# Which slot of the big pool a new tile takes: the order of the program against the times of the plan

## The chip, the cores and the metric

The kernel runs on one core of one Trainium2 chip. A core has a matrix engine (TensorE, PE in the profile, with its weight loads as PEld), three engines for elementwise work (VectorE or DVE, ScalarE or ACT, GpSimd or POOL), and SyncE (SP), which here only issues DMAs. Each engine works through its own list of instructions in the order in which they were written, and they wait for each other by semaphores. Times are microseconds (us) of the device for one execution; the figure that counts is the median over several executions. For the kernel before it is 727.84 us, from three runs between 727.78 and 729.07 us.

## The reference

One layer of a hybrid decoder on 1024 tokens of width 1024, all in float32:

```
h  = rmsnorm(x) * (1 + scale(c)) + shift(c)
cv, cg, cs, lx, ls = split(h @ w_in)                 # five blocks of 1024
v  = causal_depthwise_conv(cv * sigmoid(cg), 31 taps)
y_conv = (silu(layernorm(v)) @ pw2_w + pw2_b) * silu(cs)
xs = causal_depthwise_conv(lx, 4 taps)
r, i = sigmoid(xs @ wr + br), sigmoid(xs @ wi + bi)  # block-diagonal, 8 heads
a  = exp(-8 * r * softplus(-lam))
hs = scan: h_t = a_t h_{t-1} + sqrt(1 - a_t^2) (i_t xs_t)
y_lru = hs * silu(ls)
x  = x + (1 + gate(c)) * (concat(y_conv, y_lru) @ w_out)
out = rmsnorm(x)
```

The change leaves all of this as it is.

## The kernel before

The activations lie transposed in the on-chip memory, 128 channels by 1024 tokens to a tile of 512 KB, so each of x, v, the conv results and so on is eight tiles. A float32 product is made of three matmuls: both operands are split into a rounded part and a remainder (names with `hi` or `h`, and `lo` or `l`), and high*high, high*low and low*high are added up.

The stages follow each other in PE's list: the first four column blocks of `h @ w_in` while the inputs still arrive (`first`), the other 36 blocks with the block-diagonal gates among them (`ps`, `gate`), the lru half of `w_out` (`lp`, `lx`, `ly`), the layer norm over the convolution, the products with `pw2` (`xpw`, `zpw`, `ypw`) and with the conv half of `w_out` (`xout`, `zout`, `yout`, `y`), the last two in a scheme with seven products instead of eight. Beside this run the convolutions: five of the eight channel tiles are accumulated by DVE (`cacc`, `caccs`), three are made of products by ACT (`cq`, `co`) which GpSimd adds into `es` and `oo` with accumulating DMAs. Such DMAs also make remainders of weights and add the lru half of the output to a copy of x in HBM (`accd<-acc`).

**The plan.** Nothing is issued while the kernel text runs through these stages. Each operation is first noted in a list (class `Plan`, `op`, line 190), with its engine, an estimated cost, a priority and the buffers that it reads and writes. `Plan.order` (line 219) then plays the list through: at each planned time an engine that is free takes the ready operation of the smallest priority number, on condition that the pools have room for the buffers that it uses for the first time. A pool counts its free places in `free`. A place is taken when an operation that first uses a buffer is taken, and comes back at the planned end of the buffer's last operation (`releases`, line 255). For a DMA that end is the planned landing. `order` returns pairs of planned start and operation, sorted by planned start.

**The slots.** `Plan.run` (line 332) goes through that order. At the first use of a buffer it asks the pool of the framework for a tile, then it issues the operation. The big pool (line 351) has 47 slots of 128x1024 float32 under one tag, and the framework hands out the slot that has been unused longest in program order. 485 buffers go through these 47 slots. The plan counts how many slots are free at a planned time; which one a buffer gets is the framework's choice. The first instruction that writes a tile waits, by a semaphore, for the instructions and DMAs that last used the tile that lay in the slot before. Waits of this kind are the only thing that the choice of a slot decides.

What goes through the big pool: x, its scaled halves `uh` and `ul`, the modulation weights `modw`, all tiles of the conv and lru paths, the products `cq` and `co`, the split operands (`vha`, `vla`, `yha` and so on), the weights of the lru stage (`whi`, `wlo` from `w_out`), the combined weights of the last stages (`h34pw`, `l34pw`, ...), the running sums `acc` and `fin` and the outputs `o`. The weights of the 36 column blocks have pools of their own with two slots a name (`raw`, `whi`, `wlo`), and so have the small tiles and the accumulators of PE.

Lines that the profile names: 541 and 717 issue the matmuls of the products, 1400 those of the lru quarters, 386 and 394 the instructions of ACT, 405, 413 and 427 those of DVE, 418 GpSimd's accumulating DMAs, 432 the loads and stores of SP, 437 the stores of the output.

Of the kernel before, what the change touches and what calls it, by code (L numbers as in the profile page):

```python
# [38 lines left out]
NBIG = 47  # L39
# [60 lines left out]
FINP = -0.5  # L100
BCLATE = False
BEHIND = 0
TERMS = {**{("pw2_0", c): ("HW", "X") for c in "1z"}, **{(f"out_{p}", "1"): ("HX", "W") for p in (0, 1, 2, 3)}, **{(f"pw2_{p}", "1"): ("HX", "W") for p in (1, 2, 3)}}
LTERMS = {}
LLATE = 45
# [51 lines left out]
class Plan:  # L157
# [172 lines left out]
        return out  # L330

    def run(self):
        for _, o in self.order():
            for b in o.bufs:
                if b.tile is None:
                    pool, tag, shape, _ = self.pools[b.pool]
                    b.tile = pool.tile(shape, b.dtype, tag=tag, name=b.name)
            o.emit()

# [2 lines left out]
def hymba_layer(ctx: ExitStack, tc: tile.TileContext, xT, vecs, mod_w, w_first, w_in,  # L342
# [3 lines left out]
    act, dve, pool, pe, sp = nc.scalar, nc.vector, nc.gpsimd, nc.tensor, nc.sync  # L346
# [1 line left out]
    const = ctx.enter_context(tc.tile_pool(name="const", bufs=1))  # L348
    wpool = ctx.enter_context(tc.tile_pool(name="wpool", bufs=2))
    gwp = ctx.enter_context(tc.tile_pool(name="gwp", bufs=2))  # L350
    big = ctx.enter_context(tc.tile_pool(name="big", bufs=NBIG))
    small = ctx.enter_context(tc.tile_pool(name="small", bufs=2))
    psum = ctx.enter_context(tc.tile_pool(name="psum", bufs=3, space=bass.MemoryType.PSUM))
    psacc = ctx.enter_context(tc.tile_pool(name="psacc", bufs=2, space=bass.MemoryType.PSUM))
# [25 lines left out]
    def ACT(prio, out, in_, func, n=T, bias=None, scale=None, accum=None, r=(), w=(),  # L380
            reserve=0, after=()):
        kw = {}

        def emit():
            if func == "copy":
                act.copy(out(), in_())  # L386
                return
            if bias is not None:
                kw["bias"] = bias
            if scale is not None:  # L390
                kw["scale"] = scale
            if accum is not None:
                kw["accum_out"] = accum
            act.activation(out=out(), in_=in_(), func=func, **kw)  # L394
        ptr = sum(x is not None and not isinstance(x, float) for x in (bias, scale))
        return S.op("ACT", a_cost(n, ptr) + (0.1 if accum is not None else 0), emit, prio, r, w,
                    table=SETS.get(func), reserve=reserve, after=after)
# [26 lines left out]
    def TS(prio, out, a, s1, s2, op0, op1=None, r=(), w=(), n=0, after=()):  # L424
        kw = {} if op1 is None else {"op1": op1}
        return S.op("DVE", d_cost(n) if n else 0.2,
                    lambda: dve.tensor_scalar(out=out(), in0=a(), scalar1=s1, scalar2=s2, op0=op0,
                                              **kw), prio, r, w, after=after)
# [11 lines left out]
    def big_buf(name, dt=F32, parts=1):  # L440
        return S.buf("big", name, dt, parts)

    def part(b, a, e):
        return lambda: b()[:, a:e]

    def halves(b, a, e):
        return [(b, i) for i in range(b.parts) if i * (T // b.parts) < e
                and a < (i + 1) * (T // b.parts)]
# [7 lines left out]
    def vec(name, t):  # L456
        o = OFF[name] + t
        return V[:, o:o + 1]
# [21 lines left out]
    slots = list(FIRST + NEXT)  # L480
# [52 lines left out]
    def mm_k(prio, ps, s, xh, xl, k, cols, off=0, first=0, final=KT - 1, after=(), group="HXW", end=True):  # L533
        wh, wl = whi[s], wlo[s]
        at = LK.index(k) if s[0] == "lru" else k
        terms = [{"H": (wh, xh), "X": (wh, xl), "W": (wl, xh)}[t] for t in group]

        def emit():
            for i, (lhs, rhs) in enumerate(terms):
                for a, b in cols:  # L540
                    pe.matmul(ps()[:, a - off:b - off], k3(lhs)()[:, at, :], rhs[k]()[:, a:b],  # L541
                              start=(k == first and lhs is wh and rhs is xh
                                     and (a - off) % H == 0),
                              stop=(k == final and end and i == len(terms) - 1), skip_group_check=True)
        n = sum(b - a for a, b in cols)
        rd = [(wh, at)] * ("H" in group or "X" in group) + [(wl, at)] * ("W" in group)
        wr = []
        for a, b in cols:
            for x, ts in ((xh, "HW"), (xl, "X")):
                if any(t in group for t in ts):  # L550
                    rd += halves(x[k], a, b)
            wr += halves(ps, a - off, b - off)
        return S.op("PE", len(terms) * sum((b - a + 32) / 2400 for a, b in cols), emit, prio, rd, wr, after=after, columns=len(terms) * n)
# [6 lines left out]
    def acc_tile(name):  # L560
        return S.buf("acc", name, F32)
# [137 lines left out]
    def pair_products(name, n, w, sets, use, orders=(ORDER7,), apart=0):  # L699
# [7 lines left out]
        def product(a, b, ps, start):  # L707
            (wh, wl), xs, made = w[a], sets[b], products[name, c]
            groups = TERMS.get((name, c), ("HXW",))
            order = [(g, j) for g in groups for j in range(len(xs))]  # L710
# [128 lines left out]
    def fw_mm(prio, ps, i, xh, xl, k, cols, after=(), off=0, z=None):  # L839
        _, wh, wl = fw[k - k % 2]  # L840
        terms = ((wh, xh, 0), (wl, xh, 0), (wh, xl, 1))
        if z is not None:
            terms = terms[z:z + 1]

        def emit():
            for lhs, rhs, last in terms:
                for a, b in cols:
                    pe.matmul(ps()[:, a - off:b - off], fw_part(lhs, k, i * P, i * P + P)(),  # L848
                              rhs()[:, a:b], start=k == 0 and lhs is wh and rhs is xh,
                              stop=k == KT - 1 and bool(last), skip_group_check=True)  # L850
        n = sum(b - a for a, b in cols)
        rd, wr = [], []
        for lhs, rhs, _ in terms:
            rd.append((lhs, k % 2))
            for a, b in cols:
                rd += halves(rhs, a, b)
        for a, b in cols:
            wr += halves(ps, a, b)
        return S.op("PE", len(terms) * sum((b - a + 32) / 2400 for a, b in cols), emit, prio, rd, wr, after=after, columns=len(terms) * n)

    low = {}
    for i, ld in enumerate(LOADS):
        p = due[ld] = i - 100.0
# [5 lines left out]
        elif ld[0] in "wW":  # L869
            nk = 1 + (ld[0] == "W")  # L870
            rw, hi, lo = fw[k - k % 2]
            n, o, js = nk * FW, (k % 2) * FW, range(k % 2, k % 2 + nk)
# [17 lines left out]
    def col(t, j):  # L890
        return t[:, j:j + 1]
# [26 lines left out]
    for k in range(KT):  # L918
        p = due[f"s{k}"]
# [3 lines left out]
        else:  # L923
            dot(SCALE[k], p, KT + k, [gs_op])
        gs_op = S.op("DVE", 0.2, lambda k=k, a_=a_: dve.scalar_tensor_tensor(
            out=col(gs, k), in0=a_, scalar=col(b1, k), in1=vec("norm_g", k), op0=ALU.add,
            op1=ALU.mult), p, [("macc", KT + k), ("b1", 0)], [("gs", k)], lock=True)
        p = max(p, due[f"x{k}"], due[f"w{k}"])
# [4 lines left out]
        for a, e in START if k < UK else ((0, T),):  # L933
            n = e - a
            hk = halves(x_, a, e)
            if k == 0 == a:
                o = first_u = TS(p, part(uh, a, e), part(x_, a, e), g, None, ALU.mult, n=n,
                       r=hk + [("gs", k)], w=halves(uh, a, e))
            else:
                o = ACT(p, part(uh, a, e), part(x_, a, e), AF.Copy, n, scale=g,  # L940
                        r=hk + [("gs", k)], w=halves(uh, a, e))
# [7 lines left out]
        for ch, z in ((ch, z) for ch in (0, 1) for z in range(3 if k < ZK else 0)):  # L949
            for i, ps in enumerate(psf):  # L950
                if START[ch] in cuts[i]:
                    o = fw_mm(p + 0.1 * ch, ps, i, uh, ul, k, START[ch:ch + 1], z=z)
                    last_u[k, i, ch] = o
        for ch, (a, e) in enumerate(START):
            for i, ps in enumerate(psf):
# [3 lines left out]
                o = fw_mm(q, ps, i, uh, ul, k, ((a, e),))  # L959
# [3 lines left out]
    for k in range(KT):  # L963
        p = SQP + k
# [3 lines left out]
        for i, j in SQPAIR.get(k, ()):  # L968
            a, b = sqs[i], sqs[j]
# [33 lines left out]
    for k in range(KT):  # L1003
        p = due[f"h{k}"]
# [3 lines left out]
            out=col(shift, k), in0=a_, in1=vec("mod_shift_b", k), op=ALU.add), p,  # L1008
# [29 lines left out]
    for ch, (a, e) in enumerate(START):  # L1038
        for k in range(KT):
            p, n = TP + k + HCH * ch, e - a  # L1040
# [59 lines left out]
    held = []  # L1100
# [371 lines left out]
    for i, (s, ps) in enumerate(zip(FIRST, psf)):  # L1472
        j, p, bi = s[1] % KT, EVP + i, bias[:, i:i + 1]
        t = big_buf(f"first_u{i}", parts=4)
        for a, e in START:
            tk, pk, n = halves(t, a, e), halves(ps, a, e), e - a
# [3 lines left out]
            else:  # L1480
                late = acc_tile("late")
# [18 lines left out]
    n, started, pending_evac = 3, {}, {}  # L1500
    for s in slots[4:]:
# [41 lines left out]
        for gr, k in [(gr, k) for gr in groups for k in range(KT)]:  # L1543
            o = mm_k(n, ps, s, xh, xl, k, FULL, group=gr, end=gr == groups[-1])
# [11 lines left out]
        if s[0] == "in":  # L1556
            if s in NEXT:
                t, i = big_buf(f"next{n}", parts=2), len(FIRST) + NEXT.index(s)
# [4 lines left out]
            else:  # L1563
                o = evac_in(m, ps, n)
# [4 lines left out]
        else:  # L1569
            t = big_buf(f"acc{m}")  # L1570
# [10 lines left out]
    begun_pw2, last = [], [started[n - 1], started[n]]  # L1581
    for p in range(KT // 2):
        n = C0 + 2 * p
# [26 lines left out]
        last = [ops[0], ops[3]]  # L1610
# [5 lines left out]
    acc, n = {}, D0  # L1616
# [67 lines left out]
    for p, wout, apart in zip(OUT_P, WOUT, APART):  # L1684
        end = p == OUT_P[-1]
        n = D0 + 2 * p
        pw[p] = w = pair_weights("out", p, n, last[:1], last[1:], wout)
        n = D0 + NOUT[p]
# [17 lines left out]
        last = [ops[LASTS[p][0]], ops[LASTS[p][1]]]  # L1706
# [6 lines left out]
    n = D0 + 6  # L1713
    for prios, z, (a, e) in zip(ENDP, NPE, END[1:]):
        last_block(prios, a, e)
        norm(z, a, e)
    for o in scalings[END[1][0]][len(scalings[END[1][0]]) - BEHIND:]:
        S.hold(o, inverse[END[2][0]])
# [57 lines left out]
```

## Time and profile before

| | |
|---|---|
| runs, median | 727.84 us (727.78, 727.84, 729.07) |
| the profiled execution, its own time | 728.6 us |
| its span, first to last instruction | 726.8 us |
| granted clock of TensorE, mean | 0.996 |
| PE busy | 717.4 us (99%) |
| DVE busy | 616.5 us (85%) |
| ACT busy | 481.0 us (66%) |
| POOL busy | 170.9 us (24%) |
| DMA | 137.80 MB, mean 190 GB/s |

The profiled execution is 0.8 us longer than the median of the runs, and 1.8 us of its time lie outside of its span. A line of the waits names the engine and tile that waited, behind the arrow what ended the wait, then the total in us, the number of waits and the longest. A line of the timeline has the start, the duration, the engine, the source line, the operation with output and inputs, and in brackets the idle time of the engine before it with what ended it. Names have their buffer numbers left out, so `vla` stands for vla0 to vla3.

### The profile page before, as it was taken

To read this page: it belongs to the slowest core of one execution; us is meant where nothing else is said; L and a number is where in the kernel's file an instruction comes from. 1 tells how busy PE (TensorE), PEld (TensorE's weight loads), DVE (VectorE), ACT (ScalarE), POOL (GpSimd) and SP (SyncE) were. 2 spreads that over 40 slices of the span, in tenths; PEclk is the share of its full clock that TensorE was granted. 3 is DMA by queue.
4 is the path that set the end of the run, shared out by engine and by line. 5 is a ranking of instruction groups with operands and counts; after the bars stand their busy time and mean duration, and the time that the engine had idled before them with its cause. 6 is when DMAs were issued, how large, how long until landed. Compare 5 with 4: busy or idle time off the path is not lost.

```text
span 726.8 us, 9080 instructions
## 1 busy us (share of the span) xinstructions
PE 717.4 (99%) x3274; PEld 596.6 (82%) x3274; DVE 616.5 (85%) x848; ACT 481.0 (66%) x615; POOL 170.9 (24%) x172
## 2 busy tenths in 40 slices
PE   8999999999999999999999999999999999999996
PEld 7888888888888888888888888878888888888885
DVE  6999999889779999689499985999779766999646
ACT  7650679654779767966949779868785345745322
POOL 0035223343534230232220220111120101100003
PEclk9999999999999999999999999999999999999998
DMA  9946338758798998799999587998856946774006
GB/s 337 407 150 181 51 95 231 209 118 199 168 222 196 272 227 215 178 221 216 192 203 319 106 174 168 260 234 245 195 94 109 287 112 137 235 187 178 25 15 216
DMA packets 46059, 137.80 MB, mean 190 GB/s; under 512 B 5200, under 2 KB 15824, under 8 KB 45904
## 3 DMA queue, kind: packets, MB, share of 16 engines
q0 software_dynamic: 20016, 54.84, 42.0%
q1 hardware_dynamic: 24992, 81.48, 32.1%
q10 hardware_dynamic: 1008, 0.92, 0.4%
q8 instruction: 25, 0.41, 0.2%
q14 instruction: 18, 0.15, 0.1%
HBM read 79.37 MB, written 21.50 MB: 139 GB/s over the span
## 4 chain that ended last, share of the span: by engine, by line
PE 88%; ACT 4%; DVE 3%; issue 2%; DMA 1%; SPq 0%; DVEq 0%; ACTq 0%
PE ps L541 50%; PE xout L717 6%; PE xpw L717 6%; PE first L848 5%; PE ypw L717 3%; PE gate L1268 2%; PE lp L541 2%; PE lx L1400 2%; PE y L687 2%; PE zout L717 1%; PE zpw L717 1%; PE ly L541 1%; PE lx L541 1%; PE yout L717 1%; PE lp L1400 1%
## 5 line engine op out<-in xcount | busy, mean ns | idle before, releaser
L541 PE MATMUL ps<-uh,whi 128*128 128x512 f32 x576 | 177.4, 389 | 0.0
L541 PE MATMUL ps<-ul,whi 128*128 128x512 f32 x576 | 177.3, 389 | 0.0
L541 PE MATMUL ps<-uh,wlo 128*128 128x512 f32 x576 | 177.3, 389 | 0.0
L541 PEld LDWEIGHTS ps<-ul,whi 128*128 128x128 f32 x576 | 108.1, 188 | 22.5
L541 PEld LDWEIGHTS ps<-uh,wlo 128*128 128x128 f32 x576 | 108.1, 188 | 22.4
L541 PEld LDWEIGHTS ps<-uh,whi 128*128 128x128 f32 x576 | 108.0, 188 | 22.4
L386 ACT CAST whi<-raw 128x1024 fp32r<-128x1024 f32 (+1 forms) x44 | 45.1, 1031 | 44.1 <-PE ps L541 27.7
L418 POOL DMA_DIRECT2D es<-cq x45 | 41.0, 911 | 128.3 <-ACT cq L394 81.9
L413 POOL TENSOR_TENSOR wlo<-raw,whi 128x1024 fp32r<-128x1024 f32 x16 | 41.6, 2606 | 89.8 <-ACT whi L386 89.6
L394 ACT ACT_TABLE_LOAD x45 | 57.7, 1283 | 6.2 <-issue 2.5
L405 DVE SCALAR_TENSOR_TENSOR cacc<-v,V,cacc 128x511 f32<-128x511 f32 (+14 forms) x75 | 55.6, 741 | 0.5
L405 DVE SCALAR_TENSOR_TENSOR caccs<-v,V,caccs 128x511 f32<-128x511 f32 (+6 forms) x70 | 52.0, 743 | 2.2 <-ACT caccs L394 1.1
L405 DVE SCALAR_TENSOR_TENSOR caccs<-c,wsum,caccs 128x511 f32<-128x511 f32 (+6 forms) x70 | 52.0, 742 | 0.8
L418 POOL DMA_DIRECT2D oo<-co x39 | 37.0, 980 | 45.3 <-issue 11.9
L394 ACT ACTIVATE cq<-v,V 128x511 f32<-128x511 f32 (+14 forms) x45 | 31.7, 707 | 0.0
L405 DVE SCALAR_TENSOR_TENSOR modw<-modw,sc 128x1024 f32<-128x1024 f32 x23 | 29.5, 1286 | 2.1 <-DMA modw<-in_mod_w_dram 2.1
L405 DVE SCALAR_TENSOR_TENSOR xs<-ps,V,xs 128x1023 f32<-128x1023 f32 (+2 forms) x24 | 30.6, 1275 | 0.0
L413 DVE TENSOR_TENSOR wlo<-raw,whi 128x1024 fp32r<-128x1024 f32 x20 | 24.4, 1219 | 6.5 <-ACT whi L386 6.3
L394 ACT ACTIVATE cq<-c,wsum 128x512 f32<-128x512 f32 x42 | 29.6, 712 | 0.0
L394 ACT ACTIVATE co<-v,V 128x510 f32<-128x510 f32 (+12 forms) x39 | 26.9, 706 | 0.0
L394 ACT ACTIVATE finsq<-fin 128x512 f32<-128x512 f32 (+2 forms) x14 | 7.9, 570 | 27.6 <-DVE fin L405 14.4
L413 POOL TENSOR_TENSOR o<-fin,bc 128x256 f32<-128x256 f32 (+1 forms) x8 | 7.8, 996 | 68.1 <-ACT bc L386 68.1
(413 smaller groups left out, 1582.2 us busy)
## 6 DMA issues: line engine op xcount, KB each, us to landing
raw<-in_w_in_dram SPq DMA_DIRECT2D x36, 512.0 KB, 5.8
modw<-in_mod_w_dram SPq DMA_DIRECT2D x24, 512.0 KB, 9.2
scsd<-scs SPq DMA_DIRECT2D x8, 512.0 KB, 4.5
raw<-in_w_out_dram SPq DMA_DIRECT2D x8, 512.0 KB, 7.7
accd<-acc POOLq DMA_DIRECT2D x8, 512.0 KB, 7.3
rawpw<-in_pw_dram SPq DMA_DIRECT2D x8, 512.0 KB, 4.6
scsr<-scsd SPq DMA_DIRECT2D x8, 512.0 KB, 4.5
rawout<-in_w_out_dram SPq DMA_DIRECT2D x8, 512.0 KB, 3.5
```

The lines of the kernel that those rows point to most:

```text
L386: act.copy(out(), in_())
L394: act.activation(out=out(), in_=in_(), func=func, **kw)
L405: dve.scalar_tensor_tensor(out=out(), in0=in0(), scalar=scalar, in1=in1(), op0=op0, op1=op1, accum_out=accum)
L413: lambda: e.tensor_tensor(out=out(), in0=a(), in1=b(), op=op), prio, r, w,
L418: return S.op("POOL", ISSUE, lambda: pool.dma_start(out(), a(), accum_op=ALU.add), prio, r, w, lag=RATE * n / T, after=after, flight=flight)
L541: pe.matmul(ps()[:, a - off:b - off], k3(lhs)()[:, at, :], rhs[k]()[:, a:b], start=(k == first and lhs is wh and rhs is xh and (a - off) % ...
L687: pe.matmul(to(), half(*lhs)()[:, j * P:j * P + P], half(*rhs)()[:, c0:c1], start=a == "S1" and j == 0 and t == 0, stop=j == KT // 2 - 1 a ...
L717: pe.matmul(half(ps, 0)(), half(*lhs)()[:, j * P:j * P + P], half(*rhs)(), start=start and at == 0 and i == 0, stop=at == len(order) - 1 a ...
L848: pe.matmul(ps()[:, a - off:b - off], fw_part(lhs, k, i * P, i * P + P)(), rhs()[:, a:b], start=k == 0 and lhs is wh and rhs is xh, stop=k ...
L1268: pe.matmul(ps()[:, c0:c1], lhs()[:, j, :], rhs()[:, c0:c1], start=st == 0, stop=st == 2)
L1400: pe.matmul(half(ps, h)(), lhs()[:, o:o + P], half(*rhs)(), start=begin and j == 0 and t == 0, stop=j == NJ - 1 and t == 2, skip_group_che ...
```

## The change

The order of the operations stays as the plan makes it. `Plan.run` now picks the slot itself for the pools named in `PLACED`, which is the big pool alone. The pool is opened with one slot a tag, and 47 tags (`big0` to `big46`) take the place of 47 slots under one tag.

A first pass over the order notes for each buffer the place of its last operation in program order, the latest planned end of its operations, and that same end with `MARGINS` = 2.0 us added for DMAs (operations of SP, and GpSimd's accumulating DMAs, which have a `lag`). In the second pass the first 47 buffers take the tags in turn. Each later one looks at the slots whose holder has its last operation earlier in program order. Among these, slots whose holder has ended by the planned start of the operation go first, and among equals the one with the earliest noted end.

```
+PLACED = ("big",)
+MARGINS = 2.0
...
     def run(self):
-        for _, o in self.order():
+        out = self.order()
+        last, slots = {}, {p: [] for p in PLACED}
+        for i, (_, o) in enumerate(out):
+            for b in o.bufs:
+                late = MARGINS if o.lag or o.eng == "SP" else 0.0
+                _, end, far = last.get(b, (0, 0.0, 0.0))
+                last[b] = (i, max(o.end, end), max(o.end + late, far))
+        for i, (t, o) in enumerate(out):
             for b in o.bufs:
                 if b.tile is None:
-                    pool, tag, shape, _ = self.pools[b.pool]
+                    pool, tag, shape, cap = self.pools[b.pool]
+                    if b.pool in PLACED:
+                        held = slots[b.pool]
+                        if len(held) < cap:
+                            held.append(b)
+                            n = len(held) - 1
+                        else:
+                            n = min((z for z in range(cap) if last[held[z]][0] < i),
+                                    key=lambda z: (last[held[z]][1] > t, last[held[z]][2]))
+                            held[n] = b
+                        tag = f"{tag}{n}"
                     b.tile = pool.tile(shape, b.dtype, tag=tag, name=b.name)
             o.emit()
...
-    big = ctx.enter_context(tc.tile_pool(name="big", bufs=NBIG))
+    big = ctx.enter_context(tc.tile_pool(name="big", bufs=1))
```

## The prediction

> **What bounds the kernel now.** I read the page's totals first, then the busy time by stage, then PE's waits, and only then the waits of the other engines. The page:
>
> ```profile
> span 726.8 us, 9080 instructions
> PE 717.4 (99%) x3274; PEld 596.6 (82%) x3274; DVE 616.5 (85%) x848; ACT 481.0 (66%) x615; POOL 170.9 (24%) x172
> PE 88%; ACT 4%; DVE 3%; issue 2%; DMA 1%; SPq 0%; DVEq 0%; ACTq 0%
> ```
>
> PE holds 88% of the chain that ended last. A busy share of 99% alone doesn't say that PE runs at its pace, so the chain in order of time and the busy time by stage come next (columns there: length, then busy time and count of PE, PEld, DVE, ACT, POOL, the granted clock, the DMA share and rate):
>
> ```profile
> 120.58 81.60 PE ps L541 x360
> ...
> 0.00:12.70 12.70, 10.85 (x58) 9.41 (x58) 6.22 (x18) 8.34 (x13) 0.70 (x6) 1.00 0.86 304
> 12.70:60.00 47.30, 47.28 (x223) 39.31 (x224) 46.67 (x78) 27.43 (x40) 11.60 (x5) 1.00 0.78 294
> 60.00:414.00 354.00, 354.00 (x1571) 293.36 (x1570) 315.56 (x426) 253.28 (x318) 112.89 (x111) 1.00 0.81 190
> 414.00:475.00 61.00, 61.00 (x271) 50.40 (x269) 49.72 (x54) 53.55 (x57) 13.42 (x16) 1.00 0.86 198
> 475.00:520.00 45.00, 44.61 (x212) 36.86 (x211) 39.70 (x43) 30.82 (x38) 6.14 (x7) 1.00 0.90 239
> 520.00:717.20 197.20, 197.17 (x930) 165.25 (x929) 154.10 (x222) 106.19 (x148) 22.62 (x24) 1.00 0.55 141
> 717.20:726.80 9.60, 2.50 (x18) 2.04 (x17) 4.56 (x12) 1.39 (x5) 3.51 (x5) 0.72 0.65 219
> ```
>
> 360 matmuls in 81.60 us are 226.7 ns each, without a gap over seven column blocks. From 12.70 to 717.20 us PE's idle time is 0.02 + 0 + 0 + 0.39 + 0.03 = 0.44 us, at a granted clock of 1.00. So in 704.5 us of the span a change of waits can win 0.44 us. PE's own waits, all that the profile lists:
>
> ```profile
> PE token_stats L805 <- DVE ones L463: 1.1, 1, 1.1
> PE finbc L770 <- DVE rs65.7_0_5820 L779: 0.9, 1, 0.9
> PE first L848 <- DVE ul L405: 0.8, 1, 0.8
> PE lp L541 <- DVE yl L413: 0.3, 1, 0.3
> ```
>
> The first and third lie in the opening 12.7 us, where every big tile is a slot's first tenant, so no slot is waited for. The second is the last norm: PE needs a reciprocal, and no big tile is written between. Only the 0.3 of `lp` is in reach.
>
> **The change part by part.** It adds no instruction and moves none on any queue, SP's and POOL's among them. It changes only what the first writer of a big tile waits for. The before has such waits, and this is how one knows them: the instruction waits for something that touches none of its operands.
>
> ```profile
> DVE vla L413 <- DMA accd<-acc: 3.4, 1, 3.4
> ACT yhs L386 <- DMA es<-cq: 1.3, 1, 1.3
> ACT lnsq L394 <- DMA accd<-acc: 1.3, 1, 1.3
> ACT hlpw L386 <- DMA ylc<-yt: 1.1, 1, 1.1
> ACT xs L394 <- DMA es<-cq: 0.3, 1, 0.3
> DVE vla L413 <- PE lx L1400: 2.0, 1, 2.0
> SPq L432 <- DMA es<-cq: 18.5, 4, 9.9
> ```
>
> `vla` is made of `cr` and `vha`, and yet waits 3.4 us for a DMA that reads an `acc` tile. The new tile got that `acc` tile's slot: the last operation was issued early in the program, but its transfer was still running. Median times from issue to landing:
>
> ```profile
> accd<-acc POOLq DMA_DIRECT2D x8, 512.0 KB, 7.3
> es<-cq POOLq DMA_DIRECT2D x3, 511.5 KB, 9.6
> ```
>
> The new rule looks at the planned landing and adds 2 us, so slots last read by a DMA go to the back of the line. I expect the six DMA rows to shrink or go. What each is worth:
>
> (1) `vla`, 3.4 us on DVE. After it DVE works without a gap up to the operand that PE takes next:
>
> ```profile
> 540.43 0.69 DVE L413 TENSOR_TENSOR vla<-cr,vha 128x512 fp32r<-128x512 f32 x1 [3.37 <-DMA accd<-acc]
> ...
> 563.49 1.21 DVE L413 TENSOR_TENSOR vlb<-c,vhb 128x1024 fp32r<-128x1024 f32 x1
> ...
> 564.42 1.07 PE L717 MATMUL zpw<-vlb,whipw 128*128 128x512 f32 x4
> ```
>
> `vlb` ends at 563.49 + 1.21 = 564.70. The fourth of the `zpw` matmuls, which I take to be its reader, starts at 564.42 + 3 * 0.227 = 565.10. PE has 0.40 us to spare, so this wait costs nothing now, and without it the spare time is some 3.8 us. Worth 0. It shows how near the wait is to costing something.
>
> (2) `yhs`, 1.3 us on ACT, just ahead of PE's only wait in the middle:
>
> ```profile
> 467.41 1.05 ACT L386 CAST yhs<-sls 128x1024 fp32r<-128x1024 f32 x1 [1.31 <-DMA es<-cq]
> ...
> 471.97 1.22 DVE L413 TENSOR_TENSOR yls<-sls,yhs 128x1024 fp32r<-128x1024 f32 x1
> 473.10 0.69 DVE L413 TENSOR_TENSOR sls<-sls 128x512 f32<-128x512 f32 x1
> 473.71 0.74 DVE L405 SCALAR_TENSOR_TENSOR caccs<-v,V,caccs 128x501 f32<-128x501 f32 x1
> 474.35 2.35 DVE L413 TENSOR_TENSOR yl<-sls,yh 128x1024 fp32r<-128x1024 f32 x2
> ...
> 475.63 0.74 PE L541 MATMUL lp<-yl,whi 128*128 128x512 f32 x2 [0.29 <-DVE yl L413]
> ```
>
> DVE is back to back here with no idle time shown, so ACT's 1.3 us isn't what makes `yl` late, and PE's wait most likely stays. Between 0 and the stage's 0.39 I take 0.1, near the end that DVE's unbroken row speaks for.
>
> (3) `lnsq`, `hlpw`, `xs`: 2.7 us on ACT, in stretches where PE is idle 0.39, 0.03 and 0 us. Worth 0. What hides them is ACT's own spare time: 30.82 busy of 45.00 us, 106.19 of 197.20, and 253.28 of 354.00. Any of them would count once it lay inside DVE's unbroken row of (2).
>
> (4) SP's 18.5 us. SP issues in order, so the loads behind (weights of the next blocks, modulation weights) start earlier without it. No stage between 12.70 and 717.20 us has PE idle for more than 0.39 us, so no late load costs more than that now. Worth 0. What earlier loads bring is traffic: the DMA engines are 81 to 90% busy from 60 to 520 us, and a landing may move by some us either way. That is part of the range.
>
> (5) The waits that the rule may add. A slot freed by DVE, ACT or PE is now taken earlier, since the DMA slots have gone to the back. Whether its last reader is done on the chip depends on how well the plan's times hold. No row of the before shows such a wait, and its size is bounded by waits of the same kind: 0 from below, 2.0 us (`vla` behind PE) to 3.4 (`vla` behind a DMA) from above. A gain is excluded beyond the 0.44. I take 0, the nearest case being the column blocks, where 354.00 of 354.00 us stay busy whatever the other engines wait.
>
> A weighing by the Trainium skill, Perfetto Trace Analysis, Identifying the Most-Contended Engine: it holds that the busy share of matmuls tells little of the distance to the peak, since they are pipelined, and has one look at the share of the weight loads instead. By the rows above PEld is busy 293.36 of 354.00 us (82.9%) where PE has no gap and 36.86 of 45.00 (81.9%) in the lru stage, which is 1.0% of 45, or 0.5 us lost there instead of 0.39. By that rule the room is 0.1 us larger, and the sum would be 0.2 instead of 0.1 at best; neither reaches what can be measured.
>
> Sum: 728.6 for the profiled execution, less 0.1, is 728.5. The runs' median is 0.76 lower than that execution, so the forecast against 727.84 is 727.7.
>
> **The rivals.** About 0.2%, or 1.46 us (below 726.38, above 729.30), is what a measurement of this kernel can tell from no change; the three runs themselves lie 1.29 us apart.
>
> A, no change that can be told: 727.7, its own range 726.9 to 729.1. The ends are 727.84 less the 0.44 of PE's idle time and as much again for run to run, and the slowest run. That the change does nothing because the framework's order and the plan's mostly agree ends here too.
>
> B, faster. It needs more than PE's idle time. If besides the 0.44 the waits of 0.9 (`finbc`) and 0.8 (`first`) went, it would be 727.84 - 2.1 = 725.7. Against it: neither waits for a slot.
>
> C, slower, in the lru stage. DVE's row from 462 to 476 us is unbroken and PE already waits for it, so cover is zero: each us that `yl` or `yls` waits for a slot reaches PE whole. At the price of the `vla` row it gives 727.84 + 3.4 = 731.2, and it decides from 1.46 us on. For it: in the rows of (2) `yhs`, `yls` and two `yl` take new slots within 9 us, and slots freed by compute now come up earlier in the line. Against it: the rule takes first what the plan has free, and earliest freed first. The Trainium skill, TensorE: Matmul & The Clock Gate, What's actually happening, says that PE falls to half clock after an idle window of about 3.4 us, until another busy one; the last stretch above, with PE busy 2.50 of 9.60 us and a granted clock of 0.72, agrees. By that page C could cost another 1.7 us (an estimate, half of one window), 732.9.
>
> D, slower, by SP's order. A load of this stage waits on its slot and holds up those behind it:
>
> ```profile
> 501.80 0.33 SPq L432 DMA_DIRECT2D lsl<-lsdl  x1
> lsl<-lsdl SPq DMA_DIRECT2D x3, 512.0 KB, 4.3
> 510.45 0.40 PE L1400 MATMUL ly<-yhs,lsl 128*128 128x512 f32 x1
> ```
>
> It lands about 501.80 + 4.3 = 506.1, and PE reads such a tile at 510.45, so it has 4.3 us. A wait as long as SP's longest, 9.9, gives 727.84 + 9.9 - 4.3 = 733.4; it decides from 5.8 us on.
>
> **How the numbers follow.** A 0.65, B 0.08, C 0.19, D 0.08. A is likeliest because PE has no gap that the change could close, and because the dearest of the old slot waits stays 0.40 us short of PE. C and D together get 0.27: one late slot in a stretch without cover is enough, and the plan's times are all that guards against it. Faster 0.08, same 0.65, slower 0.27. The range runs from 726.3, just past the lower bound, to 731.2, C's price, and leaves out D, the dearer half of C and most of B.
>
> **What would show it.** Right: the row `vla <- accd<-acc` gone, `yhs <- es<-cq` and `SPq <- es<-cq` gone or smaller, DVE's idle time between 535 and 541 us down by some 3 us, PE's stretches from 12.70 to 717.20 us still within half a us of full, `lp <- yl` still there. Wrong in step (5): a new row in which `yl`, `yls`, `vlb`, or the late halves of `h34out` wait for a unit that touches none of their operands, and a PE wait behind it of over 1 us. Wrong in (4): PE or ACT waiting for `raw`, `lsl` or `cr` transfers. The prediction as a whole falls if PE's idle time in the middle rises over 1.9 us (0.44 + 1.46), or if the opening or the tail, which I leave as they are, change length.

## The result, and the profile after

The changed kernel takes 727.00 us in the median of 22 runs (726.62 to 727.67), the kernel before 728.16 us in 22 runs beside them (727.46 to 729.07). The ratio is 0.9986, with a 95% interval of 0.9980 to 0.9993: 1.16 us less, between 0.5 and 1.5. That is under the 0.2%, or 1.46 us, that the prediction called its limit, but 22 runs on either side tell it from nothing. In a later series the changed kernel took 727.44 us against 727.97 (ratio 0.9993, 0.9984 to 1.0001), so that the gain is nearer to 0.9 us than to 1.2. The forecast was 727.7 us, 0.1 us less than before, and no difference that can be told.

The changed kernel's profiled execution has a time of its own of 726.9 us. First its totals and the engines' shares of the chain that ended last:

```profile
span 725.1 us, 9076 instructions
PE 717.0 (99%) x3274; PEld 597.5 (82%) x3274; DVE 617.8 (85%) x848; ACT 480.8 (66%) x615; POOL 170.8 (24%) x172
PE 96%; DVE 1%; ACT 1%; DMA 1%; issue 0%; POOL 0%; POOLq 0%
```

Then the busy time in the same stretches as before (columns: length, busy time and count of PE, PEld, DVE, ACT, POOL, clock, DMA share, rate). The opening, the first 61 us of the lru stage with the last gates, the 45 us behind it, and the rest:

```profile
0.00:12.70 12.70, 11.54 (x63) 10.33 (x64) 8.06 (x23) 10.09 (x16) 0.70 (x6) 1.00 0.85 311
...
414.00:475.00 61.00, 61.00 (x271) 50.52 (x270) 51.09 (x55) 53.95 (x60) 12.05 (x14) 1.00 0.89 205
475.00:520.00 45.00, 44.90 (x215) 37.42 (x214) 39.34 (x42) 30.76 (x36) 7.02 (x8) 1.00 0.91 238
520.00:717.20 197.20, 196.43 (x930) 164.66 (x928) 154.47 (x226) 104.30 (x148) 23.73 (x26) 1.00 0.54 139
```

And PE's waits, all of them, with those other waits of the list that touch slots:

```profile
PE token_stats L824 <- DVE ones L482: 1.1, 1, 1.1
PE finbc L789 <- DVE rs65.7_0_5820 L798: 0.9, 1, 0.9
...
DVE vla L432 <- PE lx L1419: 1.8, 1, 1.8
...
SPq L451 <- DMA accd<-acc: 11.9, 1, 11.9
```

The waits of `vla` (3.4 us), `yhs`, `lnsq` and `hlpw` for transfers and SP's 18.5 us are gone, as foreseen; one new wait of SP came. Gone too are two of PE's four: 0.8 for `ul` in the opening and 0.3 for `yl` in the lru stage. In the 45 us from 475 on PE does 215 matmuls in place of 212. (The 0.77 us that the last row lacks are the last norm, which now begins earlier than 717.2.)

PE executes the same 3274 matmuls in the same order in both kernels, so the two traces can be laid over each other by the number of the matmul. PE is level with before at 7.5 us, 1.35 us ahead at 28 us, 1.4 ahead at 470, and 2.0 ahead from 480 on. So there are two places to explain: the opening, and ten microseconds around 475. The table gives, for every kernel that was run, the start of the 127th matmul ("opening"), the time from the 2101st to the 2141st ("lru") and from the 2521st to the 2541st ("zpw"), and the wait of `vla` for `accd<-acc`.

| kernel | opening | lru | `vla` wait | zpw | median | against before in the same series |
|---|---|---|---|---|---|---|
| before | 28.52 | 10.09 | 3.4 | 4.53 | 728.16 | |
| before again (e9) | 28.09 | 10.05 | 4.4 | 5.37 | 728.00 | +0.03 |
| changed | 27.17 | 9.46 | none | 4.53 | 727.00 | -1.16 |
| changed again (e10) | 27.37 | 9.46 | none | 4.53 | 727.44 | -0.53 |
| e1, before with r6 moved | 27.20 | 9.46 | 3.8 | 4.77 | 727.45 | -0.76 |
| e2, changed with r6 moved back | 27.01 | 10.11 | none | 4.53 | 728.09 | -0.12 |
| e3, before at other addresses | 28.08 | 10.05 | 4.3 | 5.25 | 727.96 | -0.25 |
| e4, changed at other addresses | 27.99 | 9.46 | none | 4.53 | 727.12 | -1.09 |
| e5, changed with vla2 moved back | 27.21 | 9.46 | 3.7 | 4.77 | 727.79 | -0.41 |
| e6, before with r6 and vla2 moved | 28.38 | 9.46 | none | 4.53 | 727.52 | -0.68 |
| e7, margin 6 us | 28.12 | 9.46 | none | 4.53 | 727.57 | -0.63 |
| e8, longest unused | 27.16 | 10.36 | none | 4.63 | 737.99 | +9.79 |
| e11, e8 with acc5 moved | 27.19 | 10.44 | none | 5.38 | 730.36 | +2.39 |
| e12, margin 0 | 27.51 | 9.46 | none | 4.53 | 727.03 | -0.94 |

The last column's interval is some 0.65 us to either side for the kernels within 1.2 us of before, so a single one of them says little. The stretches of the trace say more: the lru stretch takes only two values among them, 9.46 and 10.05 to 10.11.

### The profile page after: what moved, and what is told of

It is laid out like the page before. It is cut to its first block, busy times and chain, and to the rows that moved or that the text cites. A ratio compares the mean times of both kernels' runs of the same rounds, so it can differ in the third digit from the quotient of the medians.

```text
span 725.1 us, 9076 instructions
## 1 busy us (share of the span) xinstructions
PE 717.0 (99%) x3274; PEld 597.5 (82%) x3274; DVE 617.8 (85%) x848; ACT 480.8 (66%) x615; POOL 170.8 (24%) x172
## 4 chain that ended last, share of the span: by engine, by line
PE 96%; DVE 1%; ACT 1%; DMA 1%; issue 0%; POOL 0%; POOLq 0%
PE ps L560 57%; PE xout L736 6%; PE xpw L736 6%; PE first L867 5%; PE ypw L736 3%; PE gate L1287 3%; PE lp L560 2%; PE lx L1419 2%; PE zout L736 2%; PE zpw L736 2%; PE ly L560 1%; PE lx L560 1%; PE lp L1419 1%; PE yout L736 1%; PE late L867 1%; PE ly L1419 1%
```

## The experiments

**What makes the lru stretch shorter.** The ACT timeline of the kernel before, ahead of `yl` by 60 us, in the last but one round of gates; `gate` is a product of PE, `r` what ACT makes of it by a function that needs a table load:

```profile
409.12 1.28 ACT L394 ACT_TABLE_LOAD   x1
411.66 1.03 ACT L394 ACTIVATE sls<-ps 128x1024 f32<-128x1024 f32 x1 [1.25 <-PE ps L541]
414.41 1.28 ACT L394 ACT_TABLE_LOAD   x1 [1.72 <-PE gate L1268]
415.71 1.12 ACT L394 ACTIVATE r<-gate,V 128x1024 f32<-128x1024 f32 x1
...
420.26 1.23 DVE L413 TENSOR_TENSOR wlo<-raw,whi 128x1024 fp32r<-128x1024 f32 x1 [1.34 <-ACT whi L386]
```

and in the changed kernel:

```profile
410.28 1.03 ACT L413 ACTIVATE sls<-ps 128x1024 f32<-128x1024 f32 x1 [1.24 <-PE ps L560]
411.33 1.28 ACT L413 ACT_TABLE_LOAD   x1
413.00 1.12 ACT L413 ACTIVATE r<-gate,V 128x1024 f32<-128x1024 f32 x1 [0.39 <-PE gate L1287]
...
417.56 1.23 DVE L432 TENSOR_TENSOR wlo<-raw,whi 128x1024 fp32r<-128x1024 f32 x1
```

Before, ACT waits 1.72 us for PE and only then loads its table for 1.28 us. After, the load lies inside the wait and 0.39 us of waiting are left. From `sls` to `r` it is 4.05 us before and 2.72 after, 1.33 us less. DVE loses its wait of 1.34 at `wlo` and stays 1.3 us earlier, against PE's order, up to `yl`. Its three later waits for ACT in this stage are as long in the one as in the other, to 0.01 us (0.49, 2.81 and 5.87), so that the two engines hand the advance on to each other. PE's 0.29 us wait for `yl` goes, and with it the slower matmuls behind it: of the 0.63 us of the stretch 0.45 lie between the two matmuls at the wait and the rest between the next ones.

r6, the tile of that instruction, took different slots: that of cq5_10 before, that of a5 after. cq5_10 had been written by ACT and read last by a GpSimd transfer, which had landed. e1 and e2 exchange this one slot in either kernel; a list of slots by first use takes the place of the rule:

```
 # e1: the kernel before, r6 the first entry here, cq5_12 the fourth
-    44, 12, 17,  1, ...
+     1, 12, 17, 44, ...
 # and slots 1 and 44 exchanged from there on
...
-                        tag = f"{tag}{n}"
+                        tag = f"{tag}{next(nth)}"
```

> The kernel before, slot by slot and address by address, but r6 (what ACT makes of PE's gate, at 415.7 us) gets the slot that r5 held, read last by VectorE, and cq5_12, three buffers later, gets the one meant for r6, which a GpSimd transfer read last; from there on the two slots' tenants are exchanged. Table-load theory (a slot freed by a DMA puts PE's wait ahead of ACT's table load and so exposes its 1.28 us): r6 then starts about 1.3 us earlier, the table load stands ahead of PE's gate, PE's 0.3 us wait for yl in the lru stage and the gaps behind it go, PE is about 0.65 us ahead from 480 us on, span about 0.65 us under the kernel before. Rival (the removed waits for transfers on slots themselves, vla 3.4 us and yhs 1.3 us, made the gain): the r6 exchange is worth 0, and the table load stays behind PE's gate.

> The changed kernel, but r6 gets the slot that cq5_10 held (read last by a GpSimd transfer long landed) and cq5_13 gets the one of a5; from there on these two slots' tenants are exchanged. Table-load theory: the table load ahead of r6 comes again behind PE's gate, ACT loses 1.3 us there, and PE's wait in the lru stage is back: about 0.65 us slower than the changed kernel, with the opening as in the changed kernel. Rival (waits for slots): no change against the changed kernel, 727.0.

The same two instructions and what is left of PE's wait for `yl`, in e1:

```profile
411.35 1.28 ACT L427 ACT_TABLE_LOAD   x1
413.03 1.12 ACT L427 ACTIVATE r<-gate,V 128x1024 f32<-128x1024 f32 x1 [0.39 <-PE gate L1301]
```

and in e2:

```profile
412.87 1.28 ACT L427 ACT_TABLE_LOAD   x1 [1.72 <-PE gate L1301]
414.17 1.12 ACT L427 ACTIVATE r<-gate,V 128x1024 f32<-128x1024 f32 x1
...
PE lp L574 <- DVE yl L446: 0.3, 1, 0.3
```

One slot of 454 switches the whole gain of the lru stage on (10.09 to 9.46 us) and off (9.46 to 10.11). The rival falls for this stretch: e1 still has `vla`'s wait, and e2 has neither that nor `yhs`'s wait.

**Why a slot that is long free costs 1.28 us.** Both theories so far called the slot's last user, a DMA, the reason. The instructions that ACT's sequencer executes say it more exactly. An ACTIVATE carries one wait of its own; further ones stand in a waiting instruction in front of it, and in front of its table load:

| kernel | waits ahead of the table load | wait on the ACTIVATE behind it |
|---|---|---|
| before, e2 | a GpSimd transfer's, PE's | ACT's own |
| changed, e1 | DVE's | PE's |
| e7 | a GpSimd transfer's | PE's |

Before, ACT asks for three semaphores here, among them its own. Its own keeps the place on the ACTIVATE, and PE's wait moves ahead of the load, although the two others had come before. So the slot decides not only for whom the first writer waits, but also where among its waits PE's stands. It is not the number of semaphores that does it, two or three, as the expectation of e7 has it; other ACTIVATEs of the kernel before show that. The `scs` with a load at 319.80 us asks for two, PE's and ACT's own, and PE's wait stands ahead of the load there too. The `sls` with a load at 273.56 us asks for three, two transfers' and PE's, and PE's wait stays behind the load. e7 tells the place of the wait from the kind of the slot:

```
-MARGINS = 2.0
+MARGINS = 6.0
```

> The changed kernel with its margin for slots freed by transfers set to 6 us in place of 2. r6 then takes the slot of cq5_9, which a GpSimd transfer freed, but long enough ago that only this one semaphore stands beside PE's; none on ACT itself. If it is the kind of the slot that matters (freed by a DMA), r6's table load stands behind PE's gate again: about 728.1. If it is the place of PE's wait (with three semaphores, one of them ACT's own, PE's wait goes into the waiting instruction ahead of the table load; with two it stays on the instruction behind the load), the load is hidden as in the changed kernel: about 727.0.

```profile
412.29 1.28 ACT L413 ACT_TABLE_LOAD   x1
413.96 1.12 ACT L413 ACTIVATE r<-gate,V 128x1024 f32<-128x1024 f32 x1 [0.39 <-PE gate L1287]
```

The slot was freed by a DMA, and the load is hidden all the same; the lru stretch is 9.46 us. The median of 727.57 is between the two figures expected, but the trace decides. Why the ACT semaphore is asked for behind cq5_10 and not behind cq5_9 was not followed up. The Trainium skill, Perfetto Trace Analysis, Identifying Dependency Chains, says that an instruction which waits for several engines may get event-semaphore instructions in front of it. The trace agrees, and adds that these stand ahead of the table load too, at a price of 1.33 us here.

In the groups of the profile a part of the difference can be seen without a timeline, in the idle time ahead of the table loads. It falls from 6.2 to 2.0 us, and 1.72 of that are this wait; before and after:

```profile
L394 ACT ACT_TABLE_LOAD x45 | 57.7, 1283 | 6.2 <-issue 2.5
```

```profile
L413 ACT ACT_TABLE_LOAD x45 | 57.7, 1283 | 2.0 <-PEq L1787 0.7
```

**What `vla`'s wait is worth.** e5 gives the changed kernel's vla2 the slot of acc4 back; e6 gives the kernel before both good slots.

```
 # e5: the changed kernel, exchange of the slots of vla2 and vlc1
-    vla2 <- cr2     vlc1 <- acc4
+    vla2 <- acc4    vlc1 <- cr2
 # e6: e1, and vla2 <- cr2, vla3 <- yls01, ..., vlT4 <- whi45, vt2 <- acc4
```

> The changed kernel, but vla2 (the tile in front of which VectorE waited 3.4 us before) gets the slot of acc4, which it had before and which a GpSimd transfer frees, and vlc1 gets the one of cr2; from there on the two slots' tenants are exchanged. Theory of the used-up slack: the wait of 3 to 4 us on vla is back, and since PE now comes 0.65 us earlier out of the lru stage, the 0.40 us that PE had to spare before zpw no longer cover it: PE loses 0.25 us or more there and the median rises by 0.25 to 0.45 over the changed kernel, to about 727.3 or 727.4. Rival (vla's wait is worth nothing, as predicted): 727.0, with no loss at zpw.

> The kernel before at its own addresses, but with two slots settled otherwise: r6 as in e1, and vla2 in the slot of cr2, with the six tiles behind it moved on by one slot each (vt2 takes acc4's). Theory (r6's table load gives 0.65, vla's wait another 0.3 to 0.45 once PE is early): all of the gain, a median of about 727.0. Rival (the rest of the gain comes from the other 400 placements): it stays at e1's 727.45.

In e5 the wait is back at 3.7 us and the zpw stretch is 4.77 us in place of 4.53, 0.24 lost. The median rises by 0.75 us by the differences of the two series (-0.41 and -1.16), more than was expected, but by only 0.12 against the changed kernel's second series (-0.53), so the medians don't settle it. In e6 nothing is lost at zpw, and its median is 0.68 us under the kernel before, no more than e1's 0.76; the runs don't resolve the 0.2 us between these two. So `vla`'s wait can cost PE time in a trace, but the reason given, that PE now comes early, is wrong. What comes early with PE is the transfer itself: in e5 it is issued at 530.92 us in place of 532.87, 1.95 us earlier, and PE comes to its `zpw` matmuls 2.00 us earlier. The kernel before itself, run again in e9, lost more there. Its waits, DVE's and PE's rows, and the time from issue to landing of the two transfers there:

```profile
DVE vla L413 <- DMA accd<-acc: 4.4, 1, 4.4
...
540.95 0.69 DVE L413 TENSOR_TENSOR vla<-cr,vha 128x512 fp32r<-128x512 f32 x1 [4.39 <-DMA accd<-acc]
...
565.28 0.50 PE L717 MATMUL zpw<-vlb,whipw 128*128 128x512 f32 x1 [0.54 <-DVE vlb L413]
...
DMA to landing us min/median/max: 5.2/6.8/8.5
```

The same row of the prediction's execution:

```profile
DMA to landing us min/median/max: 5.4/6.4/7.4
```

The transfer on which `vla` waits took 7.4 us in the one execution and 8.5 in the other, of the same program. The longer one makes `vla`'s wait 1.0 us longer, that eats the 0.40 us to spare, and PE stands still for 0.54. The stretch is 0.83 us longer (the matmul behind the wait and some after it come slower). Over five executions with this wait, the zpw stretch loses 0, 0.83, 0.23, 0.72 and 0.24 us (before, e9, e1, e3, e5), and in the first four the loss grows with the transfer's time: 7.4, 8.5, 7.9 and 8.4 us. In e5 the transfer took only 7.5 us; there DVE needs 0.32 us more from `vla` to `vlb`, since at two places its next instruction comes 0.19 us later, as it does in the changed kernel. In all those whose vla2 has cr2's slot and no other wait came, the stretch loses nothing. How much of it the median holds is not settled: e2, without `vla`'s wait, is only 0.12 us under the kernel before.

**The opening.** e3 and e4 part the slots' tenants from the slots' addresses, since the change also orders the first 47 tiles differently in memory.

```
 # e3: list of slots of the kernel before, tags opened in order of first use
 # e4: list of slots of the changed kernel, tags opened in the kernel before's order of addresses
+        for n in OPENED:
+            pool.tile(shape, F32, tag=f"{tag}{n}", name=f"open{n}")
```

> Who follows whom in each slot is as in the kernel before, only the 47 slots lie in memory in the order of their first use, as in the changed kernel. Address theory of the opening (the transfers of the first 10 us land faster so): the opening is about 1.35 us shorter in the profile, second half of x landed by about 7.5 us, and the median is about 0.5 us under the kernel before; the lru stage is as before. Chance theory (the opening's loads land up to 2 us apart from one execution to the next, whatever the addresses): no difference in the median; the profile may show either opening.

> Who follows whom in each slot is as in the changed kernel, but the slots lie at the addresses that their first tenants had in the kernel before. Address theory of the opening: the opening is as long as before (first PE work near 10.7 us, second half of x near 9.4), only the lru stage's 0.65 us is gained. Chance theory: the same median as the changed kernel, about 1.1 us under the kernel before.

> The kernel before once more, for its opening. If the 1.35 us that the changed kernel gained there are chance (in single executions PE's 126th instruction of the record starts between 27.0 and 28.5 us whatever the slots), this execution may show either; the median is 728.2 and the 10.1 us of PE between 470.9 and 481.0 stay. If the opening belongs to the slots, it is late again, at about 28.5 us.

> The changed kernel once more. Median 727.0, 0.9 to 1.2 under the kernel before; the opening may start early or late if it is chance, and is early again if it belongs to the slots; the lru stage's stretch is 9.46 us in any case.

The opening ends between 27.0 and 28.5 us, and neither slots nor addresses sort it: e1 and e6 have the kernel before's slots and addresses for all of the first 200 tiles, and show 27.20 and 28.38; e4 has the changed kernel's tenants and shows 27.99. e3 has the changed kernel's addresses and a late opening (28.08), against the address theory; e4's late one (27.99) would fit it, but its median doesn't: -1.09 us, all of the gain. The medians of both go by the slots, as the chance theory has it. What differs is seen in PE's and DVE's rows. Before:

```profile
3.07 2.78 PE L809 MATMUL c_row<-ident,cs 128*128 128x128 f32 x16
...
10.77 1.23 DVE L405 SCALAR_TENSOR_TENSOR modw<-modw,sc 128x1024 f32<-128x1024 f32 x1 [2.14 <-DMA modw<-in_mod_w_dram]
```

The kernel before again (e9):

```profile
3.07 3.76 PE L809 MATMUL c_row<-ident,cs 128*128 128x128 f32 x16
...
6.86 0.69 DVE L405 SCALAR_TENSOR_TENSOR modw<-modw,c_row 128x512 f32<-128x512 f32 x1 [0.82 <-PE c_row L809]
...
9.52 1.21 DVE L405 SCALAR_TENSOR_TENSOR modw<-modw,sc 128x1024 f32<-128x1024 f32 x1
```

In e1:

```profile
8.99 1.23 DVE L438 SCALAR_TENSOR_TENSOR modw<-modw,sc 128x1024 f32<-128x1024 f32 x1 [0.29 <-DMA modw<-in_mod_w_dram]
```

There are two kinds of late openings. In e9 the sixteen `c_row` matmuls take 3.76 us, since all of them come 0.21 us apart, and DVE waits 0.82 us for them; before they come 0.21 us apart only up to 4.7 us and 0.11 behind that. The granted clock on record, which reaches 1.00 at 6.9 us in e9 and at 4.7 before, goes with it in thirteen of the fourteen executions: where it comes at 6.5 to 7.5 us (e3, e4, e6, e7, e9) the opening is 27.99 to 28.38, and where it comes at 4.1 to 5.5 us it is 27.01 to 27.51, but for one. That one is the profiled execution of before: the matmuls are fast, but the second half of x lands at 9.4 us and the modulation weights behind it at 10.7 (at most 7.8 and 9.0 in the others), and DVE waits 2.14. Neither kind is tied to a kernel.

**The rule itself.** e8 writes "longest unused in program order" out by hand; e11 takes one slot of it back; e12 leaves out the margin.

```
 # e8
-                                    key=lambda z: (last[held[z]][1] > t, last[held[z]][2]))
+                                    key=lambda z: last[held[z]][0])
 # e11: e8's slots as a list, with
-    acc5 <- acc4    vla0 <- yhs00   ...   vt2 <- c1
+    acc5 <- yhs00   vla0 <- yls00   ...   vt2 <- acc4
 # e12: the changed kernel
-MARGINS = 2.0
+MARGINS = 0.0
```

> The changed kernel with the rule turned back: the slot longest unused in program order, written out by hand. r6 then takes cq5_10's slot with three semaphores, as before; vla2 gets a slot freed by VectorE. By the theory of the place of PE's wait the table load is exposed again and PE waits 0.3 us for yl; vla's wait is gone but worth nothing so long as PE isn't early: about 728.1. If the gain came from the changed kernel's fewer tight slots as a whole, or from the tags, the time lies elsewhere: with the tags, 727.0.

> The kernel of e8, but acc5 gets the slot of yhs00 in place of acc4's, which a GpSimd transfer still reads, with the thirteen tiles behind it moved on by one slot each (vt2 takes acc4's). If one slot makes e8's loss (ACT waits 9.5 us for accd<-acc, PE 6.0 us for acc, and the clock falls to 0.83 behind it), about 7.5 of the 9.8 us are gone: 729.2 to 730.5, with r6's 0.6 us, the 0.7 us of xpw and what lies around it left. If many slots make it, it stays at 735 or more.

> The changed kernel without its margin for slots freed by transfers (0 us in place of 2). r6 and vla2 have the slots of the changed kernel (a5's, cr2's), r6's semaphores are the same two; vlT4 now follows acc4 by 0.1 us in the plan. If the place of r6's wait and vla's wait are what the change is worth, it gives the same 727.0 to 727.4. If the margin matters in itself, VectorE waits 3 us or more at vlT4, PE loses that beyond its slack, and the time is over 728.

e8 missed by ten microseconds: 737.99 us, a ratio of 1.0133 (1.0120 to 1.0147). Its waits and the stretch around them:

```profile
ACT acc L413 <- DMA accd<-acc: 9.5, 1, 9.5
...
PE lx L1419 <- DVE acc L424: 6.0, 1, 6.0
...
530.00:545.00 15.00, 9.02 (x34) 7.03 (x33) 6.25 (x11) 5.48 (x10) 1.78 (x2) 0.83 0.60 106
...
542.37 0.63 PE L1419 MATMUL lx<-yls,whi 128*128 128x512 f32 x1
542.80 0.63 PE L1419 MATMUL lx<-yhs,wlo 128*128 128x512 f32 x1
```

acc5 got acc4's slot while the transfer out of acc4 ran. ACT waits 9.5 us before it can empty PE's accumulator, DVE's `acc` comes behind that, PE waits 6.0 us for it, and then the next twelve matmuls follow each other at 0.43 us in place of 0.23: 2.4 us more, at a mean granted clock of 0.83 over the 15 us shown. The prediction had put 1.7 us, an estimate, on such a fall of the clock; measured it is 2.4.

e11 moves that one tile, and the same stretch is whole again:

```profile
530.00:545.00 15.00, 15.00 (x68) 12.43 (x67) 12.88 (x19) 11.45 (x17) 3.52 (x4) 1.00 0.72 128
...
PE xpw L750 <- ACT yc L427: 0.7, 1, 0.7
PE zpw L750 <- DVE vlb L446: 0.6, 1, 0.6
PE lp L574 <- DVE yl L446: 0.4, 1, 0.4
```

730.36 us, or 2.39 above before in its own series (seven runs between 729.16 and 734.21), so moving that one tile, and the thirteen behind it on by one slot, takes away some 7.4 of the 9.8 us. The last three rows, 1.7 us together, are most of what is left.

e8 also corrects the description of the kernel before. Of the 454 tiles that take a used slot (501 tiles in all, of 485 names), only 236 get in e8 the slot that they get from the framework. "Longest unused in program order" is a rough name for its rule; what it goes by was not found out. The change is worth some 0.9 us against the framework's choice, and between 10 and 11 us against that literal rule.

e12 shows that the margin of 2 us is worth nothing that can be measured here: 727.03 us, 0.94 below before, with the same r6 slot and the same 9.46 us. No kernel that was run is faster than the changed one beyond the measurement.

## Why the prediction was right, and where it was not

The change stayed under the limit that the prediction had set, 1.16 and 0.53 us against 1.46, the measured 727.00 us lies in the range, and three of its five steps stood. But the gain is real, and the forecast of it, 0.1 us, was too small by 0.4 to 1.1 us; "a gain is excluded beyond the 0.44" is wrong. That the time came out only 0.7 us from the 727.7 is in part luck, since the 727.84 that it starts from was low: 22 runs give 728.16. Of what was missed, 0.63 us are step (2)'s; whether step (1)'s part reaches the median is open.

Step (2) failed. It took 0.1 us and said that PE's wait for `yl` most likely stays, because DVE is back to back ahead of it and `yhs`'s wait on ACT isn't what makes it late. That about `yhs` is right: e2 has no such wait, and the lru stretch stays at 10.11 us. But the row was followed back only to 462 us. Its lateness was made at 415.7 us, by r6's slot, and the two engines carry it from there. No wait in the lists showed it as a slot wait: the row said `<-PE gate`, an operand of the instruction, and so the prediction's way of knowing slot waits (a wait for something that touches no operand) couldn't find it. Its cost lay in the order of wait and table load. It measured 0.63 us. The row `lp <- yl`, which the prediction named as a sign that it is right, is gone.

That is also more than the 0.39 us that step (2) gave as the stage's end, and with e9's zpw the bound of 0.44 us for all of the middle falls too. PE's busy time counts the slower matmuls behind a wait as busy. The weighing by the Trainium skill (Perfetto Trace Analysis, Identifying the Most-Contended Engine) gave an estimate of 0.5 us from the weight loads, 81.9% against 82.9%; after the change they are busy 37.42 of 45.00 us, 83.2%. Its figure was nearer to the 0.63 than the 0.39 of PE's idle time.

Step (1), worth 0, was right for the profiled execution and wrong for the kernel. The 0.40 us to spare were read from one execution, in which the transfer took 7.4 us. In e9 it took 8.5 and PE lost 0.54 us at that very place, 0.83 with the slower matmuls behind it.

Steps (3) and (4), worth 0, held: the waits of `lnsq` and `hlpw` and SP's 18.5 us are gone, and nothing in the traces laid over each other moves at their places. The new wait of 11.9 us on SP costs nothing either. Step (5), worth 0, held for this rule, since no new wait of PE came. Its sentence that no row of the before shows a wait on a slot freed by an engine overlooks one that it lists itself, `vla` behind PE's `lx`, 2.0 us; after the change it is 1.8. For another rule step (5) didn't hold: e8 is what rival C describes, a late slot in a stretch without cover, though at `acc` and not at `yl`, and dearer, 6.0 + 2.4 us.

The opening, which the prediction left as it is, was 1.35 us shorter in the profile, and it had named that as something that would make it fall. By the fourteen executions it is chance between executions and nothing of the change.

## What to carry to other kernels

A tile's slot decides more than a wait: a further semaphore that its first writer has to ask for can push the one that matters ahead of work that would have hidden it, here a 1.28 us table load. Where an engine's wait for an operand stands in front of a table load, look whether the instruction behind the load asks for the engine's own semaphore. Spare time that is read from one execution and guarded by a DMA is not safe when it is less than that DMA's spread, here 0.4 us against 1.0. And of the slots that a DMA still read, the one whose next writer empties PE's accumulator cost most here.

## What the runs showed of the hardware that was not expected

A satisfied semaphore can cost time by its place: ACT's own, which had already come, kept the place on the ACTIVATE, PE's wait stood ahead of the table load, and ACT was 1.33 us late. The granted clock reached 1.00 between 4.1 and 7.5 us into the span, from one execution to the next. The same accumulating transfer of 512 KB took between 7.4 and 8.5 us from issue to landing in executions of one and the same program. After a stop of PE of 6.0 us twelve matmuls came at 0.43 us in place of 0.23, 2.4 us in all. And the first 28 us of the kernel differ by 1.5 us from one execution to the next, more than the whole change is worth.
